# Storing each output block as a lower and an upper half of the partitions

## The chip, the cores and the metric

The kernel runs on one core of a Trainium2 chip. The metric is the time on the device in microseconds (us); the figure for a kernel is the median of several runs. The profile shows one execution, with the time from its first to its last recorded event as the span.

## The reference

`x` is 16 x 512 x 1024, `weight` is 1024 x 768, `bias` has 768 values, `residual` and the output are 16 x 512 x 768, all float32:

```python
def reference(x, weight, bias, residual):
    return (np.matmul(x, weight) + bias + residual).astype(np.float32)
```

So 61.88 MB are read from HBM and 25.17 MB are written.

## The kernel before

The 8192 rows of `x` (batch times m) are cut into 8 groups of 1024 rows. Within a group, partition p of SBUF holds the 8 consecutive rows 8p to 8p+7, so a partition's share of a group is one unbroken run in HBM: 32 KB of `x`, 24 KB of `residual`, 24 KB of the output. All of it lives in one large SBUF tensor `data`, with four slots of 24 KB per partition for residual rows and two of 32 KB for `x`; the later groups reuse slots.

The engines work as follows. ACT casts `x` to bf16 (`cast_x`, L114) and moves part of the transposed blocks (`move_blocks`, L119). DVE transposes 32 x 32 blocks (L136, L142). PE multiplies (L275, L277) into PSUM. DVE adds the product to the residual rows in place (`evacuate`, L148), and POOL adds the bias in place (`add_bias`, L190). The rows then stand finished in the residual's slot, and the store takes them from there.

All transfers are issued by SP in one hand-written order, and all of them at line L257:

```python
ORDER = ("x0a w0 w1 bias x0b r0 x1a x1b r1 x2a x2b r2 x3a x3b r3 x4a x4b st0 st1 r4 x5a x5b r5 "
         "st2 x6a x6b r6 x7a x7b r7 st3 st4+ st6 st7a st7b st7c ").split()
```

A name such as `x3a` is the first half of group 3's rows of `x` (128 partitions by 16 KB), `r3` its residual (128 by 24 KB), `st3` its store (128 by 24 KB). `st4+` stores groups 4 and 5 in one transfer (two runs of 24 KB per partition); `st7a`, `st7b` and `st7c` store 4, 2 and 2 of group 7's eight rows per partition. That makes nine stores, each of 128 partitions. SP goes through the list one by one and waits ahead of a transfer where it must:

- a store waits until POOL has added the bias to its rows (semaphore `add`), and the last one until DVE has finished (`ev`);
- `r4` and `r5` go into slots that st0 and st1 empty, so they wait for the semaphores `st0` and `st1` at 16, the count that one transfer adds when it has landed;
- `x` loads of group 2 and later wait until ACT has cast what stood in their slot, and `r7` waits for the casts of group 6;
- a load that uses the same semaphore as an earlier one waits until that one has landed (`load_into`, with the wait at L73).

Stores from st3 on share the semaphore `st`; the variable `stored` counts what they will add, and SP's last wait is for that count. A transfer that has been issued runs on its own, so several of them can be in the queue.

Of the kernel before, what the change touches and what calls it, by code (L numbers as in the profile page):

```python
# [10 lines left out]
P = 128  # L11
# [10 lines left out]
@with_exitstack  # L22
def kernel(
    ctx: ExitStack,
    tc: tile.TileContext,
    x: bass.AP,
    weight: bass.AP,
    bias: bass.AP,
    residual: bass.AP,
    out: bass.AP,  # L30
):
    nc = tc.nc
    with tc.tile_critical(name="all", no_gpsimd_drain=True), ExitStack() as es:  # L33
        emit(nc, es, x, weight, bias, residual, out)


def emit(nc, es, x, weight, bias, residual, out):
# [11 lines left out]
    sp, act, dve, pool, pe = nc.sync, nc.scalar, nc.vector, nc.gpsimd, nc.tensor  # L49
# [17 lines left out]
    def sem(name):  # L67
        if name not in sems:
            sems[name] = es.enter_context(nc.semaphore(name))
        return sems[name]  # L70

    def wait(eng, name, value):
        eng.wait_ge(sem(name), value)  # L73
# [14 lines left out]
    def group(ap, g):  # L88
        return ap[g * G * P:(g + 1) * G * P, :].rearrange("(p j) k -> p j k", p=P)

    def span(start, size):
        return data[:, start:start + size] if isinstance(start, int) else data[:, bass.ds(start, size)]

    def x_half(g, half):
        return span(X0 - (g % 2) * X_SLOT + half * (B * K), B * K).rearrange("p (t k) -> p t k", k=K)

    def r_home(g):

        return (g % 4) * R_SLOT + ((g + 1) // n_grp) * (X0 - 3 * R_SLOT)

    def r_rows(start, j, n):
        return span(start + j * N, n * N).rearrange("p (j n) -> p j n", n=N)
# [103 lines left out]
    landed, stored = {}, 0  # L206

    def load_into(name):

        before = landed.get(name, 0)  # L210
        landed[name] = before + 16
        if before:
            wait(sp, name, before)
        return name

    for name in ORDER:
        into = name
        if name == "bias":
            wait(sp, "ev", EV0)
            src, dst = bias[None, :].to_broadcast((P // Q, N)), bias_rows[0:P:Q, :]  # L220
        elif name[0] == "w":
            k0 = int(name[1]) * (R // 2)
            src, dst = w_rows[:, k0:k0 + R // 2, :], w_stage[:, k0:k0 + R // 2, :]
        elif name[0] == "x":
            g, part = int(name[1]), name[2:]
            j0, j1 = PARTS[part]
            if g > 1 and part == "a":
                wait(sp, "cast", 2 * (2 * g - 2))
            if g == 3 and part == "a":
                wait(sp, "wc", 2)  # L230
            into = load_into(name[0] + part)
            src, dst = group(x2d, g)[:, j0:j1, :], x_half(g, j0 // B)
        elif name[0] == "r":
            g = int(name[1])
            if g == n_grp - 1:
                wait(sp, "cast", 2 * (2 * g))
            elif g > 3:
                wait(sp, f"st{g - 4}", 16)
            into = load_into("r")
            src, dst = group(res2d, g), r_rows(r_home(g), 0, G)  # L240
        else:
            g, part = int(name[2]), name[3:]
            n = 2 if part == "+" else 1
            j0, j1 = (LAST_PARTS if g == n_grp - 1 else PARTS)[part.strip("+")]
            end = (g + n - 1) * G + j1
            if end == n_sub:
                wait(sp, "ev", ev_end)
            else:
                wait(sp, "add", added[end - 1])
            src, dst = r_rows(r_home(g), j0, j1 - j0), group(out2d, g)[:, j0:j1, :]  # L250
            if n > 1:
                src = span(r_home(g), n * R_SLOT).rearrange("p (g k) -> p g k", g=n)
                dst = out2d[g * G * P:(g + n) * G * P, :].rearrange(
                    "(g p j) n -> p g (j n)", g=n, p=P)
            if g > 2:
                into, stored = "st", stored + 16
        sp.dma_start(out=dst, in_=src).then_inc(sem(into), 16)  # L257
    wait(sp, "st", stored)

# [2 lines left out]
    with pe.Fori(0, n_bat) as b:  # L262
        mv.wait()
        tm.wait()
        for i in range(B):
# [4 lines left out]
            for k in range(R):  # L270
                lhsT = words[:, k // 2, k % 2, :]
                for c, (n0, nl) in enumerate(chunks):
                    dst, rhs = po[:, i, n0:n0 + nl], w_sb[:, k, n0:n0 + nl]
                    if c == 0:
                        ins = pe.matmul(dst, lhsT=lhsT, rhs=rhs, start=(k == 0), stop=(k == R - 1))  # L275
                    else:
                        ins = pe.add_instruction(mybir.InstMatmult(  # L277
                            name=nc.get_next_instruction_name(),
# [34 lines left out]
```

## Time and profile before

| | |
|---|---|
| median of 3 runs | 210.47 us (210.4 to 210.62) |
| the profiled execution | 210.49 us |
| its span | 208.7 us |
| DMA | 87.05 MB in 5176 packets, 417 GB/s over the span |
| PE busy | 170.1 us (82%) |
| DVE busy | 166.3 us (80%) |
| ACT busy | 154.0 us (74%) |
| POOL busy | 115.5 us (55%) |
| stores: issue to landing, median | 23.9 us (3 MB, five of them), 31.1 (6 MB), 10.1 (1.5 MB), 8.6 (768 KB, two) |

Times within the execution count from the start of the span. The row DMA of the page gives the mean busy share of the core's 16 DMA engines in 40 equal slices, in tenths, and the row GB/s what they moved. An engine's busy share says how long it worked, not whether anyone waited for it. Time from issue to landing contains the time that a transfer stood behind others in the queue. The trace also holds a record of each packet that a DMA engine moved (its start, its duration and its size) and of the moments at which a transfer's completions arrived.

### The profile page before, as it was taken

The numbers are of one execution on the slowest core, as the hardware profiler recorded it, in microseconds if no ns is written. First come the engines' busy times: TensorE is split into PE (matmuls) and PEld (weight loads), VectorE is DVE, ScalarE is ACT, GpSimd is POOL, SyncE is SP. The second block draws the span as 40 slices with busy tenths as digits, with TensorE's granted clock in tenths as the row PEclk, the third lists the DMA queues.
The fourth block names the chain that finished last, engine by engine and source line by source line (L and its number), as shares of the span: only waits on it lengthen the run. The fifth ranks groups of instructions, "written<-read, shape, count | busy, mean of one in ns | idle before, by whom it ended". The sixth has DMA issues, their size and how long they took to land.

```text
span 208.7 us, 2836 instructions
## 1 busy us (share of the span) xinstructions
PE 170.1 (82%) x1024; PEld 50.5 (24%) x512; DVE 166.3 (80%) x180; ACT 154.0 (74%) x168; POOL 115.5 (55%) x38
## 2 busy tenths in 40 slices
PE   0000399999999999999999999999999999999800
PEld 0000123332332233323322333233323222223200
DVE  1009686899989998999899989998999899983500
ACT  0365997697989799979997998889897989720000
POOL 0055002918484757566665757484839392999700
PEclk9999999999999999999999999999999999999965
DMA  6999999999999999999999999999999999999993
GB/s 207 433 427 455 414 427 446 454 404 408 449 415 436 443 414 436 443 447 391 443 443 405 451 410 447 413 436 430 429 429 446 429 405 452 443 424 410 436 415 139
DMA packets 5176, 87.05 MB, mean 417 GB/s; under 512 B 564, under 2 KB 564, under 8 KB 824
## 3 DMA queue, kind: packets, MB, share of 16 engines
q1 hardware_dynamic: 5176, 87.05, 97.9%
HBM read 61.88 MB, written 25.17 MB: 417 GB/s over the span
## 4 chain that ended last, share of the span: by engine, by line
DVE 30%; ACT 22%; issue 16%; DMA 15%; PE 10%; ACTq 1%; DVEq 1%; SPq 0%
DVE xt L142 17%; DMA data<-in_x_dram 15%; ACT xt L119 12%; ACT xb L114 8%; DVE tq L136 7%; PE po L275 7%; DVE data L148 6%; PE po L277 3%; ACT L114 2%; DVEq L84 1%; ACTq L84 0%; ACTq L114 0%; ACTq L124 0%; DVEq L148 0%; SPq L308 0%
## 5 line engine op out<-in xcount | busy, mean ns | idle before, releaser
L275 PE MATMUL po<-w_sb,xt 128*128 128x512 bf16 x512 | 169.2, 383 | 27.1 <-DVE xt L142 24.1
L190 POOL TENSOR_TENSOR data<-data,bias_bc 128x1536 f32<-128x1536 f32 x32 | 109.8, 3454 | 68.9 <-DVE data L148 68.7
L277 PE MATMUL po<-w_sb,xt 128*128 128x256 bf16 x512 | 140.6, 275 | 0.0
L119 ACT COPY xt<-tq 32x512 uint32<-32x512 uint32 x128 | 78.9, 617 | 20.1 <-DVE tq L136 17.3
L142 DVE STREAM_TRANSPOSE xt<-xb 32x512 uint32<-32x512 uint32 x128 | 90.2, 704 | 2.7 <-ACT xb L114 0.7
L275 PEld LDWEIGHTS po<-w_sb,xt 128*128 x512 | 50.5, 99 | 146.3 <-issue 144.4
L148 DVE TENSOR_TENSOR data<-po,data 128x1536 f32 (+2 forms) x33 | 56.0, 1709 | 12.4 <-PE po L277 11.9
L114 ACT CAST xb<-data 128x2048 bf16 x32 | 64.9, 2077 | 0.3
L136 DVE STREAM_TRANSPOSE tq<-xb 128x1024 uint32<-128x1024 uint32 x16 | 19.8, 1235 | 1.6 <-ACT xb L114 1.6
L114 ACT ACT_TABLE_LOAD x8 | 10.3, 1283 | 9.8 <-DMA data<-in_x_dram 9.6
L185 POOL CAST w_sb<-data 128x3072 bf16<-128x3072 f32 x2 | 5.5, 2744 | 12.8 <-DMA data<-in_weight_dram 12.8
L153 DVE LOAD_MASK_SELECT bias_bc<-bias_rows x1 | 0.0, 14 | 14.0 <-DMA bias_rows<-in_bias_dram 14.0
L150 DVE MEMSET bias_rows<- 128x768 f32 x1 | 0.7, 698 | 1.2 <-SPq L33 1.2
L153 DVE STREAM_SHUFFLE bias_bc<-bias_rows 128x768 f32<-128x768 f32 x1 | 1.0, 1005 | 0.0
L297 POOL MEMSET const-float32-0.0<- 128x1 f32 x1 | 0.1, 98 | 0.2 <-issue 0.2
L297 POOL MEMSET const-bfloat16-1.0<- 128x1 bf16 x1 | 0.1, 101 | 0.0
L297 POOL MEMSET const-uint8-127<- 128x1 uint8 x1 | 0.1, 101 | 0.0
L297 POOL MEMSET const-float32-1.0<- 128x1 f32 x1 | 0.1, 98 | 0.0
## 6 DMA issues: line engine op xcount, KB each, us to landing
data<-in_x_dram SPq DMA_DIRECT2D x16, 2048.0 KB, 17.1
data<-in_residual_dram SPq DMA_DIRECT2D x8, 3072.0 KB, 17.1
out_dram<-data SPq DMA_DIRECT2D x5, 3072.0 KB, 23.9
out_dram<-data SPq DMA_DIRECT2D x1, 6144.0 KB, 31.1
data<-in_weight_dram SPq DMA_DIRECT2D x2, 1536.0 KB, 12.3
out_dram<-data SPq DMA_DIRECT2D x1, 1536.0 KB, 10.1
out_dram<-data SPq DMA_DIRECT2D x2, 768.0 KB, 8.6
bias_rows<-in_bias_dram SPq DMA_DIRECT2D x1, 12.0 KB
```

Of the source, the lines that this page charges most:

```text
L84: self.eng.reg_add(self.reg, self.reg, self.step)
L114: act.copy(out=xb[:, c], in_=part.rearrange("p t (a j r) -> p t j a r", j=R // 2, r=2)).then_inc(sem("cast"), 1)
L119: act.copy(out=xt[q * Q:(q + 1) * Q, half, :, :, m * Q:(m + 1) * Q], in_=tq[m * Q:(m + 1) * Q, :, :, q]).then_inc(sem("mv"), 1)
L136: dve.transpose(out=tq[:], in_=xb_words(0)).then_inc(sem("tq"), 1)
L142: ins = dve.transpose(out=xt[q * Q:(q + 1) * Q, half, :, :, m * Q:(m + 1) * Q], in_=words[m * Q:(m + 1) * Q])
L148: dve.tensor_add(out=rt, in0=po[:, j % 4:j % 4 + n, :N], in1=rt).then_inc(sem("ev"), 1)
L150: dve.memset(bias_rows[:], 0.0).then_inc(sem("ev"), EV0)
L153: dve.stream_shuffle(out=bias_bc[:], in_=bias_rows[:], mask=[0] * 32).then_inc(sem("bb"), 1)
L185: pool.tensor_copy(out=w_sb[:, part, :], in_=w_stage[:, part, :]).then_inc(sem("wc"), 1)
L190: pool.tensor_add(out=rt, in0=rt, in1=bias_bc[:, None, :].to_broadcast((P, 2, N))).then_inc(sem("add"), 1)
L275: ins = pe.matmul(dst, lhsT=lhsT, rhs=rhs, start=(k == 0), stop=(k == R - 1))
L277: ins = pe.add_instruction(mybir.InstMatmult(name=nc.get_next_instruction_name(), ins=[pe.lower_ap(rhs), pe.lower_ap(lhsT, for_matmul_weig ...
```

## The change

Each store is issued as two transfers, one of partitions 0 to 63 and one of partitions 64 to 127, right after one another and on the same semaphore. Each half has 64 rows, which are dealt to the 16 DMA engines as four rows each, where a whole store gives each engine eight. The counts that are waited for grow from 16 to 32: for `r4` and `r5`, and in the sum `stored` for the last wait. Loads, compute and the order of the list stay as they are.

```diff
@@ -235,7 +235,7 @@
             if g == n_grp - 1:
                 wait(sp, "cast", 2 * (2 * g))
             elif g > 3:
-                wait(sp, f"st{g - 4}", 16)
+                wait(sp, f"st{g - 4}", 32)
             into = load_into("r")
             src, dst = group(res2d, g), r_rows(r_home(g), 0, G)
         else:
@@ -253,7 +253,10 @@
                 dst = out2d[g * G * P:(g + n) * G * P, :].rearrange(
                     "(g p j) n -> p g (j n)", g=n, p=P)
             if g > 2:
-                into, stored = "st", stored + 16
+                into, stored = "st", stored + 32
+        if name[0] == "s":
+            sp.dma_start(out=dst[:P // 2], in_=src[:P // 2]).then_inc(sem(into), 16)
+            src, dst = src[P // 2:], dst[P // 2:]
         sp.dma_start(out=dst, in_=src).then_inc(sem(into), 16)
     wait(sp, "st", stored)
```

## The prediction

> **What bounds the kernel now.** I read the DMA rows of the page first, because the change touches nothing but stores.
>
> ```profile
> PEclk9999999999999999999999999999999999999965
> DMA  6999999999999999999999999999999999999993
> GB/s 207 433 427 455 414 427 446 454 404 408 449 415 436 443 414 436 443 447 391 443 443 405 451 410 447 413 436 430 429 429 446 429 405 452 443 424 410 436 415 139
> ...
> q1 hardware_dynamic: 5176, 87.05, 97.9%
> HBM read 61.88 MB, written 25.17 MB: 417 GB/s over the span
> ```
>
> The 16 DMA engines are busy from the first slice to the last. Each moves 87.05 / 16 = 5.44 MB in 97.9% of 208.7 us, which is 204.3 us, so 26.6 GB/s per engine. No engine of the core is as full (PE 82%, DVE 80%), and PE's clock is full until its work ends. Next come the stretches, to see whether stores and loads go at one pace (columns: stretch, length, five engines' busy time, PE clock, DMA share, GB/s).
>
> ```profile
> 35.00:56.00 21.00, 20.57 (x128) 6.17 (x63) 18.54 (x21) 17.86 (x21) 13.79 (x4) 1.00 1.02 437
> ...
> 171.00:181.00 10.00, 9.57 (x59) 2.84 (x29) 9.85 (x11) 8.59 (x11) 5.86 (x3) 1.00 1.01 433
> 181.00:191.00 10.00, 10.00 (x63) 3.03 (x31) 7.12 (x8) 3.03 (x5) 9.86 (x4) 1.00 1.00 430
> ...
> 198.00:207.50 9.50, 0.00 (x0) 0.00 (x0) 0.24 (x1) 0.00 (x0) 0.00 (x0) 0.58 0.75 316
> ```
>
> Before 72 us there are only loads, after 170.1 us (r7 has landed) only stores: 437 against 430 to 433 GB/s, the same. In the last row compute is over and transfers alone set the end; the final store was issued at 198.3 us and landed at 207.4. Last, who waits for stores:
>
> ```profile
> SPq L257 <- DMA out_dram<-data: 24.6, 2, 17.0
> ...
> SPq L73 <- DMA out_dram<-data: 8.8, 1, 8.8
> ```
>
> The first are loads into slots that a store empties, r4 above all (17.0 us); the second is SP's last wait, for the last store. The chain of waits names compute (DVE 30%, ACT 22%) for much of the span. But compute ends at 198.24 us with about 9 us of stores still to move, and the transfers have no gap before. So the end is the sum of all transfer time: what a store gains or loses per row arrives at the end one for one.
>
> The trace's packet records give the price of a row on an engine: 24,576 bytes take 0.912 us, 12,288 take 0.460, 6,144 take 0.234, back to back, each row of a transfer one packet. Loads and stores agree (24,576-byte loads 0.912 to 0.920).
>
> **The change part by part.** All of it is on SP and the DMA queue; PE, DVE, ACT and POOL keep their instructions and order.
>
> *Nine more issues on SP.* A store issue takes 0.338 us in the median, so 9 x 0.338 = 3.0 us of SP time. They stand ahead of r4, x6a and, at the end, of each other. SP spends over 100 us waiting, and the queue holds about 7 us of work when the last store is issued: cover for 0.34 us each. Were the cover gone, only the last one would reach the end, 0.34 us. I take 0.
>
> *Nine more completions per engine.* Each transfer ends on each engine with a 4-byte packet of about 9 ns (next row's start 6 ns later). 9 x 0.009 = 0.08 us per engine, all on the path. I take +0.1.
>
> *Waits for 32 instead of 16.* r4 and r5 wait for both halves, which is the same last row as before; the final wait counts all. 0. The splits release nothing earlier, since nobody waits for a half.
>
> *The same rows dealt otherwise.* This is the whole case. A store today gives each of 16 engines 8 of 128 rows; after, 4 of the lower 64 and then 4 of the upper 64. Bytes per engine and row sizes are unchanged. Store time per engine now: 56 rows x 0.912 (st0 to st3, st4+, st6) + 8 x 0.460 (st7a) + 16 x 0.234 (st7b, st7c) = 51.07 + 3.68 + 3.74 = 58.5 us. No transfer in the trace has 64 rows on 16 engines, so I bound it.
>
> [...] Each row takes twice as long: +58.5 us. Lower end: the engine is the limit, rows still take 0.912 us: 0, or a small gain (rival C, -1.9).
>
> Which row is it nearest to? [...] Chaining the packets by end and start gives 16 rows of work, and one of these engines is slower in one kind of work only: from 170 to 198 us its 24,576-byte store rows take about 0.945 us while its loads just before take 0.912 to 0.921, and the other 15 engines store at 0.912. Its rows return to normal (0.460, 0.234) once compute has ended. An engine that was its own limit would not depend on direction and on what else runs; something on the stores' path is already at its limit with one engine on it. So I take the upper end, two engines sharing one path at half pace.
>
> [...]
>
> A little comes off. [...] The completion records of a store put 15 of the 16 engines within 0.3 us to 0.5 us of each other, so a pair that is 0.05 to 0.1 us apart, the closest pair, which ends last, saves that at each of 18 halves: 0.9 to 1.8. I take -1.1. Sum: 58.5 + 0.1 - 1.1 = +57.5.
>
> *What is late next.* With st0 and st1 each 7.3 us longer, x5a lands at 116.1 + 14.6 = 130.7 us, then with st2 also, x6a at 140.8 + 21.9 = 162.7 and r7 at 170.1 + 21.9 = 192.0. Compute follows its loads closely (ACT already waits 1.0 us for an x load), so its end moves from 198.2 to about 220. The stores behind r7 (15.7 MB, 36 us now, 73 then) last until about 265. So the compute delay of 22 us is covered, and the queue stays filled: when SP waits for st0, st1 is behind it; when r7 is released by the casts of group 6, x7b still has some 6 us to run.
>
> The profiled execution took 210.49 us (span 208.7 and 1.79 around it), 0.02 from the median of 210.47. 210.5 + 57.5 = **268.0 us**, a span of 266.2.
>
> **The rivals.**
>
> B, the engine is the limit. Two engines on neighbouring rows do not meet; +0.1, 210.6 us. For it: one pace for all sizes and both directions. Against: the engine that is slow in stores alone. It is also what comes out if the change doesn't spread as it says, with the lower half's rows all on eight engines and the upper half's on the other eight: the halves then run side by side, each engine with its own 8 rows as today. The listing of SP's instructions shows two 64-row transfers each, not the engines. [...]
>
> C, faster: the deal evens out the slow engine. Its 56 long store rows are about 0.03 us too long each: 1.7 us, and the records agree, the last store's first engine lands at 205.4 us and the last at 207.4. If the cause lies with its rows in SBUF, half of those rows now go to a partner: 0.9 to 1.9 us off, 209.1 us taken. It decides only if sharing itself is free, that is if a path carries twice an engine's pace, which its slowing under one engine speaks against.
>
> D, the sharing is real but smaller. D1: one partner is always served first, so the pair drifts apart by one half-store (4 x 0.912 = 3.65 us; 8 rows for st4+, 7.3) and never meets again: 214 to 218 us. D2: the lane carries more than one engine's pace; at 1.6 times, a row takes 2 / 1.6 = 1.25 times as long, +14.6, 225 us; at 1.5 times +19.5, 230 us; at 1.1 times +48, 258 us. No row shows a packet faster than 26.9 GB/s, so I see no sign of spare, only that it can't be excluded.
>
> **How the numbers follow.** Forecast A 0.75, B 0.08, C 0.08, D1 0.04, D2 0.05. A's own range is 262 to 272: down for pairs further apart (18 halves x 0.3 us = 5.4), up for no offset (+1.1), the slow engine's 1.7, and about 1 us of idling at the new waits. The range that holds 8 in 10 takes in A and D2: 225 to 272. A measurement here tells about 0.2% (0.4 us) from no change. Faster is C, 0.08; same is B, 0.08; slower is A and D, 0.84.
>
> **What would show it.** Right: the long store rows near 1.82 us instead of 0.912 and the load rows unchanged at 0.611 to 0.920; DMA share still at 9 tenths, but near 217 GB/s in the store stretches (all of the last 70 us) and 430 in load stretches; PE, DVE and ACT idle for some 20 us in the middle, waiting for x5 and x6; compute ending near 220 us. The prediction is wrong if store rows stay at 0.912 us (B, or C when the last engine's lag also shrinks), if only the first store is slow and the pairs then land several us apart (D1), or if rows lie between 1.0 and 1.7 us (D2). It is also wrong in its sum, not its mechanism, if DMA shows idle slices, which would mean that compute or SP holds stores back and the 22 us is not covered.

## Result and the profile after

| | before | stores in halves |
|---|---|---|
| median of 4 runs each | 210.45 us | 244.05 us (242.16 to 249.8) |
| ratio | | 1.1565, 95% interval 1.1458 to 1.1671 |
| profiled execution | 210.49 us, span 208.7 | 249.8 us, span 248.0 |

The change costs 33.6 us. The forecast was slower by 57.5 us, 268.0 us in all: sign and cause came out, the size did not. This kernel's runs spread by 3%, so ratios, here and below, leave out runs over 1.5% above the fastest of their kernel, which medians keep (without the longest run the median here is 242.61 us, +32.2). The profiled run is that longest one: its times below show mechanisms, and sizes are taken from the medians.

The page's DMA rows after the change:

```profile
DMA  7999999999999999999999999999999999999830
GB/s 254 425 425 458 414 445 420 419 424 435 436 436 420 425 338 242 234 254 313 424 436 427 420 313 357 452 427 404 411 384 317 274 230 262 254 345 282 260 125 19
...
q1 hardware_dynamic: 5320, 87.05, 94.8%
HBM read 61.88 MB, written 25.17 MB: 351 GB/s over the span
```

DVE, ACT and POOL are as busy as before (PE 177.2 us against 170.1), with the same bytes and 144 packets more (nine completions on 16 engines). Up to the first store nothing differs. Then the rate has holes down to 230 GB/s, while loads alone still get 420 to 450. The last two slices, 125 and 19 GB/s, are new: most engines have run out of work and a few still have some.

The stretches of the same execution say where the holes lie (last three columns: PE clock, DMA share, GB/s):

```profile
80.00:90.00 10.00, 9.95 (x62) 3.03 (x31) 9.70 (x11) 9.30 (x11) 6.55 (x2) 1.00 1.00 426
90.00:100.00 10.00, 9.52 (x59) 2.83 (x29) 9.84 (x12) 8.58 (x12) 6.85 (x2) 1.00 1.01 236
...
120.00:130.00 10.00, 6.00 (x28) 1.55 (x14) 4.05 (x3) 0.56 (x2) 3.40 (x2) 0.74 1.00 429
...
200.00:210.00 10.00, 9.95 (x63) 3.03 (x31) 6.89 (x7) 2.79 (x5) 9.86 (x4) 1.00 1.01 261
...
230.00:240.00 10.00, 0.00 (x0) 0.00 (x0) 0.00 (x0) 0.00 (x0) 0.00 (x0) 0.50 0.63 209
```

At 90 to 100 us st0 goes out at 236 GB/s, with the DMA engines full: each row simply takes longer (1.906 to 1.909 us for many of them, as shown below). At 120 to 130 us loads run at 429 GB/s while ACT, at 0.56 us of 10, waits for x5a. The waits agree, first SP's, then ACT's, and last ACT's line of the kernel before:

```profile
SPq L260 <- DMA out_dram<-data: 32.2, 2, 21.8
...
SPq L73 <- DMA out_dram<-data: 22.2, 1, 22.2
```

```profile
ACT L114 <- DMA data<-in_x_dram: 26.8, 4, 9.4
```

```profile
ACT L114 <- DMA data<-in_x_dram: 9.6, 2, 8.6
```

r4 waits 21.8 us for st0 (17.0 before), SP's last wait is 22.2 us (8.8 before), ACT waits 26.8 us for `x` loads (9.6 before). None of these sets the end: compute is over at about 217 us, and 31 us of stores follow.

The packet records show the price itself. Under st0 many long store rows (24,576 bytes) take 1.906 to 1.909 us where they took 0.912, and of the rows that start in 95 to 100 us 93% are slow (over 1.3 times 0.912). Later stores hold both kinds: 44% slow rows at 190 to 195 us, 98% at 195 to 200, 24% at 215 to 220. Summed over an engine, 24,576-byte rows rose from 109.8 to 137.8 us, and all rows together by 30.7 us. The other 8.5 us of the 39.3 by which this execution's span grew are engines without work: at 230 us all 16 still move rows, at 237 us nine, from 244 us one. The completion records show what grew besides: the 16 engines finish st0's first half within 0.6 us, its second within 1.5, st1's halves within 2.5 and 4.0, and a load such as x6a within 9.3.

### The profile page after: what moved, and what is told of

The parts are those of the page before. It is cut to its first block, busy times and chain, and to the rows that moved or that the text cites. A ratio compares the mean times of both kernels' runs of the same rounds, so it can differ in the third digit from the quotient of the medians.

```text
span 248.0 us, 2829 instructions
## 1 busy us (share of the span) xinstructions
PE 177.2 (71%) x1008; PEld 51.7 (21%) x512; DVE 166.4 (67%) x180; ACT 153.6 (62%) x168; POOL 115.5 (47%) x38
## 4 chain that ended last, share of the span: by engine, by line
DMA 36%; DVE 17%; PE 14%; ACT 12%; issue 8%; DVEq 1%; ACTq 0%; SPq 0%
DMA data<-in_x_dram 36%; DVE xt L142 10%; PE po L278 9%; ACT xb L114 6%; ACT xt L119 5%; PE po L280 5%; DVE data L148 4%; DVE tq L136 3%; ACT L114 1%; DVEq L84 0%; ACTq L84 0%; ACTq L114 0%; ACTq L124 0%; DVEq L148 0%; DVEq L155 0%
## 5 line engine op out<-in xcount | busy, mean ns | idle before, releaser
L278 PE MATMUL po<-w_sb,xt 128*128 128x512 bf16 x496 | 172.5, 396 | 38.0 <-DVE xt L142 24.1
L190 POOL TENSOR_TENSOR data<-data,bias_bc 128x1536 f32<-128x1536 f32 x32 | 109.8, 3448 | 87.6 <-DVE data L148 87.5
L280 PE MATMUL po<-w_sb,xt 128*128 128x256 bf16 x512 | 144.1, 281 | 0.8
L119 ACT COPY xt<-tq 32x512 uint32<-32x512 uint32 x128 | 78.9, 617 | 22.1 <-DVE tq L136 19.3
L278 PEld LDWEIGHTS po<-w_sb,xt 128*128 x512 | 51.7, 101 | 163.8 <-issue 162.5
L114 ACT ACT_TABLE_LOAD x8 | 10.3, 1283 | 26.9 <-DMA data<-in_x_dram 26.8
L185 POOL CAST w_sb<-data 128x3072 bf16<-128x3072 f32 x2 | 5.5, 2745 | 12.8 <-DMA data<-in_weight_dram 12.8
```

Of the source, the lines that this page charges most:

```text
L114: act.copy(out=xb[:, c], in_=part.rearrange("p t (a j r) -> p t j a r", j=R // 2, r=2)).then_inc(sem("cast"), 1)
L119: act.copy(out=xt[q * Q:(q + 1) * Q, half, :, :, m * Q:(m + 1) * Q], in_=tq[m * Q:(m + 1) * Q, :, :, q]).then_inc(sem("mv"), 1)
L185: pool.tensor_copy(out=w_sb[:, part, :], in_=w_stage[:, part, :]).then_inc(sem("wc"), 1)
L190: pool.tensor_add(out=rt, in0=rt, in1=bias_bc[:, None, :].to_broadcast((P, 2, N))).then_inc(sem("add"), 1)
L280: ins = pe.add_instruction(mybir.InstMatmult(name=nc.get_next_instruction_name(), ins=[pe.lower_ap(rhs), pe.lower_ap(lhsT, for_matmul_weig ...
```

## The experiments

Theory 1: a lower or upper half makes two engines share one path out of SBUF and each row takes twice as long; partners that have drifted apart no longer meet, and that gives back what the prediction had too much. Its rivals: short or additional transfers cost by themselves (theory 2), or a path has some spare, so that all rows are a little slower (theory 3). All ratios are against the kernel before on the same chip.

**Two transfers, both of full height.** The second transfer is kept, the halving of the partitions undone; each transfer takes half of a partition's bytes.

```diff
-            sp.dma_start(out=dst[:P // 2], in_=src[:P // 2]).then_inc(sem(into), 16)
-            src, dst = src[P // 2:], dst[P // 2:]
...
+                h = (j1 - j0) // 2
+                cuts = [(src[:, :h], dst[:, :h]), (src[:, h:], dst[:, h:])]
+            sp.dma_start(out=cuts[0][1], in_=cuts[0][0]).then_inc(sem(into), 16)
+            src, dst = cuts[1]
```

(The lines left out cut st4+ between its two groups.)

> Two transfers per store, but each of all 128 partitions and half of each partition's bytes. Theory 1 (a lower or upper half puts two engines on one path out of SBUF; the number of transfers is free): each engine keeps its rows, so 210.5 us plus the longer sum of two 12,288-byte rows against one of 24,576 (0.920 against 0.912 us, 56 times 0.008 = 0.45) plus 0.1 for completions: 210.5 to 211.3. Theory 2 (the second transfer itself costs, by issue, completion or waits for two): as the changed kernel, 240 to 245.

Measured: 211.34 us against 210.48, ratio 1.0039 (1.0025 to 1.0053). The nine issues, nine completions per engine, waits for 32 and shorter rows cost 0.9 us together, a little above what theory 1 had. Theory 2 is out: 32.7 of 33.6 us belong to the choice of partitions.

**Only st0 in halves.**

```diff
+        cuts = [slice(0, 64), slice(64, P)] if name == "st0" else [slice(0, P)]
...
+        for cut in cuts:
+            sp.dma_start(out=dst[cut], in_=src[cut]).then_inc(sem(into), 16)
```

(This is done to the kernel before, with r4's wait raised to 32. The next two runs differ from this one in the line `cuts` and in that wait alone.)

> Only st0 goes in halves, the other eight stores whole. Theory 1, with partners in step at the first split store and drifting apart later: the full price of one store, 7.3 us, less what the partners already drift within it (st0 landed 5.4 us later than before in the changed kernel): 215.5 to 217.8 us. Theory 3 (the price is evenly smaller because a path carries more than one engine's pace): a ninth of 33.6 us, 3.7 us, 214.2 us, and rows near 1.4 us. If a path is never shared: 210.5.

Measured: 217.11 us, ratio 1.0319 (1.0302 to 1.0336), +6.6 us. That is nearly the 7.3 us of the prediction for one store, and not the ninth part of 33.6. The stretches of its execution over st0, and then two of the same stretches in the kernel before:

```profile
91.00:94.00 3.00, 3.00 (x21) 0.88 (x9) 2.94 (x5) 1.75 (x4) 3.00 (x2) 1.00 1.12 262
94.00:97.00 3.00, 3.00 (x20) 0.88 (x9) 2.95 (x5) 2.88 (x6) 2.40 (x1) 1.00 0.93 197
97.00:99.00 2.00, 2.00 (x14) 0.59 (x7) 1.95 (x3) 1.97 (x3) 0.00 (x0) 1.00 1.16 221
```

```profile
91.00:94.00 3.00, 3.00 (x21) 0.88 (x9) 2.97 (x3) 1.79 (x2) 3.00 (x2) 1.00 1.14 492
94.00:97.00 3.00, 3.00 (x20) 0.88 (x9) 2.93 (x6) 2.88 (x6) 3.00 (x1) 1.00 0.94 401
```

From 91 to 99 us that is 227 GB/s in the mean, about half of the 433 of the kernel before. The 16 rows that start from 95.1 to 96.6 us take 1.906 to 1.909 us each, as two engines on one path without spare would; rows at the edges of a half lie on both sides of that, from 0.912 to 2.8 us. Theory 3, rows near 1.4 us throughout, is out. Since a window counts packets by their start, its rate swings with only some 25 long packets in it.

**Only st0, cut at 32 and 96.**

```diff
+        cuts = [slice(0, 32), slice(32, 96), slice(96, P)] if name == "st0" else [slice(0, P)]
...
```

> Only st0 is cut, into partitions 0 to 31, 32 to 95 and 96 to 127. [...] So 4 rows of the 8 are slow: +3.65 us less drift, 213 to 214.3 us, less than with st0 in halves. Theory 2 (short transfers are slow, whichever rows they have): all rows near 1.9 us and at least the time of st0 in halves, 216 or more.

Measured: 213.47 us, ratio 1.0138 (1.0122 to 1.0155), +3.0 us with three transfers, where the two halves cost 6.6.

```profile
91.00:94.00 3.00, 3.00 (x19) 0.93 (x10) 2.97 (x3) 1.79 (x2) 3.00 (x1) 1.00 1.18 467
94.00:97.00 3.00, 3.00 (x20) 0.88 (x9) 2.94 (x5) 2.88 (x6) 3.00 (x2) 1.00 0.87 197
```

From 91 to 94 us the middle 64 rows go out at full rate (rows of 0.912, a few of 0.925 to 0.972). From about 94 us it is partitions 96 to 127, and the rate drops to 197 GB/s, with rows mostly of 1.7 to 2.5 us. So the height of a transfer is not the cause: 64 rows are fast (0.912 us here) or slow (1.906 to 1.909 in halves) depending on which 64.

That four rows of an engine's eight would be slow was an estimate, and it did not fit: the first part, partitions 0 to 31, ran at 0.912 to 0.955, but for two of its 32 rows at 1.22. In the run with two halves the first two rows of each engine were fast as well (0.912 to 0.940), and the slow ones began with the third. Both follow directly behind a load (x4b). So that the time fell into the expected 213 to 214.3 us is in part luck: four slow rows per engine stood in the sum, and only the two of the last part were slow.

**Only st0, in eight transfers of 16 partitions.**

```diff
+        cuts = [slice(i, i + 16) for i in range(0, P, 16)] if name == "st0" else [slice(0, P)]
...
```

> Only st0 is cut, into eight transfers of 16 neighbouring partitions, one row per engine. [...] If only pairs of engines meet: as st0 in halves, 216 to 218. If a path is never shared: 210.5 to 211.

Measured: 224.1 us, ratio 1.0646 (1.0625 to 1.0668), +13.6 us. About twice what two halves cost. Most rows of the second transfer take 2.1 to 3.7 us, up to four times 0.912, where two engines in turn would take 1.82. But then the engines scatter: the last 16 completions are 6.8 us apart, many rows are back at 0.912, and the rows together are 10.7 us longer per engine, about half of the 21.9 us that eight rows at four times 0.912 would add (an estimate, 8 x 3 x 0.912). It was the first sign that drift counts. Four rows at 98.4 to 99.6 us take 5.9 to 6.8 us, more than four times 0.912; what they waited for was not found.

**Realigning the engines.** After each store SP waits until it has landed. This is done to the changed kernel and, as the control, to the kernel before.

```diff
         sp.dma_start(out=dst, in_=src).then_inc(sem(into), 16)
+        if name[0] == "s":
+            wait(sp, into, stored if g > 2 else 32)
```

(16 instead of 32 in the control.) The wait does two things: the engines come back into step, and the queue is empty ahead of six of the nine stores (st1, st4+, st6 and the three of group 7). st0, st2 and st3 still stand directly behind a load.

> The changed kernel, and after each store SP waits until it has landed before it issues the next transfer, so that all engines start each store together. To be read against the kernel before with the same waits. Drift theory: the difference of the two is what the prediction had, 45 to 57 us, since partners are in step at the start of each store. If the changed kernel was cheaper than predicted for another reason (mixing with loads, a path with spare): the difference stays at 28 to 38 us.

> The kernel before with the same waits after each store, the control for the run above. Each wait empties the queue for about 2 us, from issue to first data and from last data to completion, and the loads behind st0, st1 and st2 come later: 225 to 240 us by any theory.

Measured: 275.44 us with halves (ratio 1.3081, 1.3062 to 1.3099), 225.19 us with whole stores (1.0695, 1.068 to 1.071). The difference is 50.25 us: the halves cost 16.7 us more with the waits. The control's 14.6 us are 1.6 per wait; in the kernel before, 1.0 us pass from the first issue (0.95 us) to its first packet and 0.5 from the end of the last packet (206.99) to the last completion. First the run with halves, then the control, each over stores alone:

```profile
206.00:236.00 30.00, 16.34 (x101) 4.80 (x49) 10.88 (x11) 3.10 (x6) 15.76 (x5) 0.85 0.99 210
```

```profile
190.00:201.00 11.00, 11.00 (x70) 3.33 (x34) 7.48 (x8) 3.37 (x6) 10.86 (x4) 1.00 1.00 429
```

210 against 429 GB/s, and no recovery over 30 us. The store st6 alone, from an empty queue, took 15.3 us from its first packet to its last completion (238.5 to 253.8) against 7.8 in the control: +7.5, the prediction's 7.3 for a store in step. st1 (+7.4) and st4+ (+15.2, twice the bytes) paid the full price too.

The three stores behind a load did not, though that load's completions lie within 1.1 us: from them to the store's own last one it is 12.1, 11.2 and 11.5 us for st0, st2 and st3, against 7.3 each in the control, so +4.8, +3.8 and +4.2. Their first rows run at 0.912 us again.

Nor are the 16.7 us the price of drift alone. Summed over an engine, the rows of st6's lower half, from an empty queue, are 4.06 us longer than at 0.912, those of its upper half, directly behind, 3.21, and the changed kernel's queue was not empty ahead of these stores. All runs of this kernel lie within 0.3 us, where the changed kernel's spread by 7.6, which fits engines that drift differently from run to run.

**Setting the partners apart on purpose, first try.** st0 is cut so that eight engines should get 10 rows and eight 6, by estimate a lag of about one half-store (4 x 0.912 = 3.65 us); st4+ becomes st4 and st5.

```diff
...
+            if name == "st0":
+                cuts = [slice(i, 32, 4) for i in range(4)] + [slice(32, 96), slice(96, P)]
...
```

> Stores in halves as in the changed kernel, except that st0 is cut so that engines 0 to 7 get 10 rows and engines 8 to 15 get 6 (partitions 0 to 31 as four transfers of 8 rows, every fourth partition; 32 to 95; 96 to 127), and groups 4 and 5 are stored one after the other. That sets the partners about 4 rows, 3.65 us, apart, one half of a store. Theory 1: from then on a partner is in the other half, on another path, and rows take 0.912 us: 2 rows more on the fuller engines (1.8 us), 1.8 for the shared outer rows of st0 and about 2 in the shorter last stores: 213 to 218 us, with nearly all the 33.6 us gone. If partners do not matter, or if drift is not what gave back 24 us: 238 us or more.

Measured: 235.41 us, ratio 1.1082 (1.1057 to 1.1108). Better than the changed kernel, far from the 213 to 218 us expected. From 98 to 110 us, around st1, 75% of the rows were slow again. Since the halves of st1 could still have met the rest of st0, I repeated it with the lag made long before the first store.

**Second try, and its control.** The uneven deal is moved to the two weight loads, once with stores in halves and once whole; st4+ is again st4 and st5 in both.

```diff
+        if name[0] == "w":
+            cuts = [slice(i, 32, 4) for i in range(4)] + [slice(32, 96), slice(96, P)]
...
```

> The changed kernel, with the two weight loads at the start dealt unevenly (partitions 0 to 31 as four transfers of every fourth partition, which go to engines 0 to 7; then 32 to 95; then 96 to 127), and groups 4 and 5 stored one after the other. Engines 0 to 7 move 4 rows of 12,288 bytes more than engines 8 to 15 in each weight load, so they fall 2 x 4 x 0.460 = 3.7 us behind, one half of a store, long before the first store. Theory 1 (an engine of 0 to 7 and one of 8 to 15 meet on a path, and only while both are in the same half): the halves no longer meet, 210.5 + 1.8 for the fuller engines + about 2 in the shared weight rows + about 2 in the short last stores, 213 to 219 us. If the pairs are others, or if the lag is lost at the first store: 228 to 245 us.

> The same uneven weight loads with whole stores, the control for the run above. Theory 1: every engine keeps its own path in whole stores, so only the fuller engines and the shared weight rows cost: 211.5 to 215 us. The difference of the two is the price of the halves with partners set apart: 0 to 5 us by theory 1, 15 us or more otherwise.

Measured: 249.78 us (ratio 1.1865, 1.1812 to 1.1918) with halves, 219.04 us (1.04, 1.0381 to 1.0419) with whole stores. The first is above everything that was expected of it. The control cost more than the 1 to 4.5 us expected: w1 landed at 23.5 us instead of 15.9. The difference between the two is 30.7 us, so nearly the full price of the halves remained. The lag itself was there: of x2b's 16 completions eight came at 58.4 to 58.8 us and eight at 61.4 to 61.7. The stretches around st0:

```profile
93.00:96.00 3.00, 3.00 (x21) 0.93 (x10) 2.94 (x4) 2.93 (x4) 0.00 (x0) 1.00 1.02 328
96.00:99.00 3.00, 2.56 (x17) 0.69 (x7) 3.00 (x3) 2.44 (x2) 2.22 (x1) 1.00 1.26 328
99.00:110.00 11.00, 11.00 (x70) 3.32 (x34) 10.29 (x12) 10.15 (x11) 7.46 (x3) 1.00 1.00 232
```

From 93 to 95 us only the eight engines that are ahead are in st0's lower half; the other eight still move x4b, at 0.611 to 0.619 us a row as ever. Yet most of the store rows already take 1.28 to 2.28 us. So, if slow rows mean a shared path, these eight meet each other: partners lie within a group of eight and not, as I had assumed, one in each. That part of theory 1 is refuted. Which engine shares with which, the records don't say, as they carry no engine number.

**Loads in halves.** The residual loads go as two transfers, the stores whole; the waits on `r` count 32.

```diff
+        if name[0] == "r":
+            sp.dma_start(out=dst[:P // 2], in_=src[:P // 2]).then_inc(sem(into), 16)
+            src, dst = src[P // 2:], dst[P // 2:]
...
```

> The eight residual loads go in halves, the stores whole. Theory 1 with paths that limit writes into SBUF as they limit reads: the same bytes as the stores (25.2 MB), rows near 1.9 us at first, then drift; 230 to 255 us. If only the way out of SBUF is shared: 210.5 to 211.

Measured: 273.59 us, ratio 1.3001 (1.2961 to 1.3041), +63.0 us, above the whole range expected.

```profile
22.00:35.00 13.00, 11.08 (x57) 3.16 (x29) 8.46 (x12) 9.85 (x12) 0.00 (x0) 1.00 0.95 202
36.00:44.00 8.00, 6.30 (x41) 1.85 (x19) 3.42 (x2) 3.19 (x2) 5.92 (x2) 1.00 1.00 426
80.00:85.00 5.00, 5.00 (x33) 1.47 (x15) 4.91 (x7) 3.38 (x7) 5.00 (x2) 1.00 0.98 210
```

202 GB/s in r0's halves, 426 in the `x` loads, 210 again in r3's: halves slow loads as they slow stores (197 to 262 GB/s under st0 alone). And here the engines stay in step: up to 175 us the completions of a half lie at most 0.8 us apart, against up to 9 us in the changed kernel. No row is spared here: 1023 of the 1024 half rows are slow, 1.849 us in the mean, so 64 of them cost an engine 64 x (1.849 - 0.912) = 60.0 us; with the 2.9 us by which the other rows grew, that is the measured time.

## Why the prediction was right or wrong

- **Transfers bound the end, so a slower row arrives there one for one.** Right. DMA is full up to the last slices, compute is done 31 us before the end, and its wait for x5a and x6a is covered.
- **Issues, completions and waits cost about 0.1 us.** Near: full-height pairs of transfers cost 0.9 us, of which 0.45 was expected from the shorter rows alone.
- **The choice of the upper end, two engines at half pace.** Right, and by 4.6% low in price: 1.908 us for a row instead of 2 x 0.912 = 1.824. That a row takes twice as long was an estimate that no run showed then; the runs showed 1.906 to 1.909 us for a store row where the slowing is steady, and 1.849 in the mean for a load row. That two engines on one path are behind it fits these figures and was not shown by itself. One store from a standing start cost +7.5 us for 7.3 worked out, one store in the kernel's own order +6.6.
- **The reason for that choice.** It was read off one engine that was 3.5% slower in stores alone. That the choice of partitions sets the pace is now shown by the middle 64 rows, 0.912 us against 1.906 to 1.909 in halves; what slowed that one engine was not tested.
- **"A little comes off", -1.1 us.** This is the term that failed. No run shows what it rests on, that a pair meets only while both are in the same half; two groups of eight engines set 3 us apart still paid 30.7 us. The sum was 57.5 and the result 33.6, so 23.9 us more came off. Two things were left out of it. First, every row was charged double from its start, but the first rows of a store directly behind a load are not: even in step, st0, st2 and st3 cost +12.8 us together instead of 21.9. That 9.1 us is more than the 7.2 by which the run with the waits (50.25) stays below 57.5; longer pauses at its waits, 3.1 us more idle than in the control, make up part of the difference. Second, partners were taken to keep their 0.05 to 0.1 us. They came apart from the second half on, 1.5 us after one store and 4 to 9 us later, and many store rows then ran at 0.912. In the profiled execution the last six stores, behind r7, add 22.1 us instead of the 36.6 worked out, the first three 17.2 instead of 21.9. How much of the 16.7 us between the two runs is drift was not measured by itself. By an estimate it is about 9: the six lower halves that start from an empty queue pay some 5 us for that (0.85 for st6, as above), and 3 us are idling.
- **Rival D1** had the drift, but in one step and for good (214 to 218 us). In fact it neither stops the meeting nor stays: slow rows go from 44% to 98% and down to 24% within the last stores. **Rivals B and C** need all rows at 0.912 us and are out; so is **D2**, since rows do not settle at a value between: where the sharing is steady they take 1.906 to 1.909 us.
- **The range, 225 to 272 us,** held the result only because it took in D2 as well, whose mechanism did not occur. The forecast's own part of it, 262 to 272, lay 18 us too high, so that is luck.
- **The sign of a wrong sum that I named, idle DMA slices,** appears only in the last slices. They are stragglers, the last engine stopping some 16 us after the first, and not compute holding back stores, since compute ended at 217 us, near the 220 worked out.

## What to carry to other kernels

Where transfers set the end, look at which partitions a transfer covers, not only at how many bytes and issues it has: a cut through the bytes of all 128 partitions cost 0.9 us here, the same cut into lower and upper partitions 33.6, and of the residual loads 63.0. When a price per row is multiplied up, ask which rows pay it: here the first rows behind a load did not, and engines that had scattered paid less than engines in step (by estimate some 9 of the 16.7 us between the two runs), though setting two groups of eight apart on purpose did not help (30.7 us still). The spread of a kernel's times can be a hint of it: 7.6 us over four runs here, where the engines scatter, against 0.3 with the waits.

## What the runs showed of the hardware that I had not expected

- Where the slowing is steady, a store row takes 1.908 us. If two engines share a path then, that is 25.8 GB/s for 2 x 24,576 bytes, where one alone gets 26.9 (0.912 us a row): 4.4% are lost on top.
- The first two rows per engine of a store that follows a load ran at 0.912 to 0.940 us although the rows behind them, in the same half, took up to 2.1; from an empty queue (st6 with the waits) the first row already took 1.77 to 1.92 us. What spares the rows behind a load was not tested.
- The engines drift apart in stores cut into halves (0.6 to 9 us) but hardly in loads (at most 0.8 us up to 175 us). Why the two directions differ stays open. In loads the first rows of a half were slow too: 1023 of 1024 rows were.
